# Loading the bias rows of all but the last pair of neighbourhood heads during the window heads

## The chip, the cores and the metric

The kernel runs on one core of one Trainium2 chip, in one launch. The metric is the device time of the launch in microseconds, the median of several executions. A profiled execution of the same kernel gives the trace; its own time and the span of its core (first to last instruction) are given below.

## What is computed

A trunk of two layers over 512 tokens of width 1024, float32 throughout. Each layer projects the normalised tokens once and feeds two kinds of attention heads, eight of each: heads of kind A (a window of blocks along the sequence, two heads of keys, rotary positions) and heads of kind B (each token looks at a neighbourhood of the 8 x 64 grid, with a learned bias by relative position). The change touches only how the bias of kind B reaches the chip.

```
def neighbourhood_attn(q, k, v, rel_bias):
    ...
    bias = rel_bias[:, dr_i[:, None, None, :, None], dc_i[None, :, :, None, :]]
    bias = jnp.where(valid[None, None, :, :, None, :], bias.astype(jnp.float32), NEG)
    ...
    scores = jnp.einsum('brjqhd,brjwkhd->bhrjqwk', qg, kb).astype(jnp.float32) * (HEAD_DIM ** -0.5)
    scores = scores + bias[None]
    ...
    p = jax.nn.softmax(scores.reshape(shp[:-2] + (wr * B_KBAND_C,)), axis=-1).reshape(shp)
    out = jnp.einsum('bhrjqwk,brjwkhd->brjqhd', p.astype(v.dtype), vb)

for l in range(DEPTH):
    h = rms_norm(x, attn_norm_g[l])
    z = jnp.einsum('bsd,dc->bsc', h, w_in[l])
    qa, ka, va, qb, kb, vb, ga, gb = jnp.split(z, IN_SPLITS, axis=-1)
    ...
    mixed = jax.nn.sigmoid(ga) * ya + jax.nn.sigmoid(gb) * yb
    x = x + jnp.einsum('bsd,de->bse', mixed, w_out[l])
    ...
    x = x + jnp.einsum('bsf,fd->bsd', u, w_down[l])
```

## The kernel before

Every product is split into a high and a low part of each operand and made of three matmuls of the type float32r. TensorE therefore has long rows of matmuls of the projections (tiles named `mm`, one PSUM bank each), and between them stand the short matmuls and transposes of the heads (tiles named `at`). All buffers in SBUF are cut from two arenas, one for float32 and one for float32r, so the profile knows them only as `arena`.

The order of the instructions is found when the program is built. The function `layer` yields one small unit of projection matmuls after another, and after each unit a driver may advance one of several generators ("chains"): one for each pair of heads (`chain_pair_a`, `chain_pair_b`), one for each head (`chain_heads`, which calls `head`). A chain goes on when its `Need` is met: given keys have been set, and by a planner's clocks the operands are ready. Each engine then carries out its own list strictly in that order. Since all calls go through one recording helper, nearly every row of the profile bears line L305.

The steps that matter here:

- `k_parts` makes the keys of a pair of heads. Two casts on ScalarE and two subtractions on VectorE (64 x 512 each) write the high and low keys of each head in half of the partitions, and four DMA issued by SyncE copy them to the other half (`arena<-arena`, 64 x 512, 128 KB each). The first score matmuls of a head wait for its two copies. It is called once for all heads of kind A, and once for each pair of kind B, so there are five groups of four copies in a layer.
- `bias_load` brings the bias of one head with 16 DMA issued by SyncE, of 8 KB each, so a pair takes 32 (`arena<-in_rel_bias_b`). A completion semaphore of SyncE's DMA is shared by every eighth one, so each of them waits until the one eight places ahead has landed.
- `bias_mask` adds the mask to the loaded bias with three additions on VectorE, when the head begins.

SyncE issues its DMA in the order of the program: a copy that stands behind a row of bias loads is issued only after the last of them. In this kernel the first pair's bias is requested at the end of the last pair of kind A, and each further pair's right behind the copies of keys of the pair ahead of it. `biases` is a list with one entry in it at a time.

Of the kernel before, what the change touches and what calls it, by code (L numbers as in the profile page):

```python
# [209 lines left out]
def trunk(ctx: ExitStack, tc: tile.TileContext, a: dict, out: bass.AP, lay: Layout):  # L210
# [20 lines left out]
    def buf(shape, dtype=F32):  # L231

        n = int(np.prod(shape))
        x = lay.place(n, dtype)
        t = arenas[dtype][:, x : x + n]
        if len(shape) == 2:
            t = t.rearrange("p (a b) -> p a b", b=shape[1])
        elif len(shape) == 3:
            t = t.rearrange("p (a b c) -> p a b c", b=shape[1], c=shape[2])
        return t  # L240
# [4 lines left out]
    def act(dtype=F32):  # L245
        return buf([S], dtype)
# [727 lines left out]
    def q_parts(tiles, col, res, scale=None):  # L974

        yield Need("pe", tiles, [at_slots])
        ps = turned(tiles, col, ident) if scale is None else turned_back(tiles, col)
        for own, other in HALVES:
            yield Need("act", [ps])
            q = act(F32R)  # L980
            if scale is None:
                yield from gsplit(held(ps[own]), by_columns(q[own]), by_columns(q[other]))
            else:
                yield from gsplit(ps[own], q[own], q[other], scale=scale[own])
            res.append(q)
        at_slots.give(clock["dve"])

    def k_parts(tiles, col, perm, res, in_a=False):

        dst, src = (by_columns, held) if in_a else (lambda t: t, lambda t: t)  # L990
        yield Need("pe", tiles, [at_slots])
        ps = turned(tiles, col, perm)
        for own, other in HALVES:
            yield Need("act", [ps])
            kh, kl = act(F32R), act(F32R)
            yield from gsplit(src(ps[own]), dst(kh[own]), dst(kl[own]))
            res.append((kh, kl))
        at_slots.give(max(clock["dve"], clock["act"]))
        for (own, other), (kh, kl) in zip(HALVES, res[-2:]):
            yield Need("dma", [kh, kl])  # L1000
            Q.dma_start(kh[other].bitcast(F32), kh[own].bitcast(F32))
            Q.dma_start(kl[other].bitcast(F32), kl[own].bitcast(F32))

    def v_parts(src, v):

        yield from gsplit(src, v[:, :, TOP], v[:, :, BOT])
# [117 lines left out]
    def bias_load(l, h):  # L1124

        t = buf([8, 32])
        src = a["rel_bias_b"]
        base = (l * 8 + h) * 15 * BW + 8
        for half in range(2):
            for r in range(8):  # L1130
                p = 64 * half + 8 * r
                Q.dma_start(
                    t[p : p + 8],
                    bass.AP(tensor=src.tensor, offset=base + r * BW + 8 * half, ap=[[1, 8], [BW, 8], [1, 32]]),
                )
        return t

    def bias_mask(t):

        bm = buf([2, 2, S // 4])  # L1140
        for i, n, k0 in ((0, 2, 0), (2, 1, 1), (3, 1, 0)):
            o = bm.rearrange("p e k (a n) -> p (e k a) n", n=64)[:, 2 * i : 2 * (i + n)]
            m = cst[:, C_MB + 16 * i : C_MB + 16 * (i + n)].rearrange("p (d c) -> p d c", c=8)
            b = t[:, :, 16 * k0 : 16 * (k0 + n)].rearrange("p r (d c) -> p d r c", c=8)
            V.tensor_tensor(
                o.rearrange("p d (r c) -> p d r c", c=8), b, m.unsqueeze(2).to_broadcast([P, 2 * n, 8, 8]), ALU.add
            )
        return lambda j: bm[:, int(j == 0)].rearrange("p k n -> p (k n)")
# [28 lines left out]
    def layer(l):  # L1177
# [68 lines left out]
        def chain_pair_a(hp):  # L1246

            keys = [f"qa{l}", f"ka{l}"] + ([f"{key}scores{2 * hp - 3}"] if hp > 1 else [])
            yield Need(keys=keys)
            qs = []  # L1250
            yield from q_parts(qa, P * hp, qs)
            oa.append(act())
            for i in range(2):
                h = 2 * hp + i

                def make(res, h=h, i=i, o=oa[-1]):
                    res += [
                        qs[i], k_a[h // 4], v_a[h // 4], mask_a, ident, nsnk[:, l, h : h + 1],
                        snk[:, l, h : h + 1], o[HALVES[i][0]], True,
                    ]  # L1260
                    yield Need()

                makes[h] = make
            if hp == 3:
                biases.append([bias_load(l, i) for i in range(2)])
            done.add(f"{key}pair{hp}")

        biases = []

        def chain_norm_b(half):  # L1270
            yield Need(keys=[f"qk{l}{half}"])
            f = []
            yield from head_scale(qk[half], 8, nrm.rst, f)
            for b in range(NB):
                yield Need()
                normalise(qk[half][b], f[0], b, 8)
            done.add(f"{key}norm{half}")

        def chain_pair_b(hp):

            g0 = 8 + 2 * hp
            raw, col = qk[hp // 2], P * (hp % 2)
            keys = [f"v{l}", f"{key}norm{hp // 2}", f"{key}scores{g0 - 3}"]
            if hp:
                keys += [f"{key}bias{g0 - 1}"]
            yield Need(keys=keys)
            rb = biases.pop()
            qs, ks = [], []
            yield from q_parts(raw, col, qs, scale=gb[:, l : l + 1])
            yield from k_parts(raw, 4 * HD + col, ident, ks)  # L1290
            if hp < 3:
                biases.append([bias_load(l, 2 * hp + 2 + i) for i in range(2)])
            ob.append(act())
            for i in range(2):
                h = 2 * hp + i

                def make(res, h=h, i=i, o=ob[-1]):
                    v = buf([NB, P], F32R)
                    yield Need("dve", [rb[i]])
                    bias = bias_mask(rb[i])  # L1300
                    done.add(f"{key}bias{8 + h}")
                    yield Need("act")
                    yield from v_parts(vb[:, :, HD * h : HD * h + HD], v)
                    res += [qs[i], ks[i], v, bias, rev, 3e38, None, o[HALVES[i][0]], False]
                    yield Need()

                makes[8 + h] = make
            done.add(f"{key}pair{4 + hp}")
# [28 lines left out]
        for hp in range(4):  # L1337
            spawn(chain_pair_a(hp))
            spawn(late(2 * hp))
            spawn(late(2 * hp + 1))  # L1340
        for hp in range(4):
            if hp % 2 == 0:
                spawn(chain_norm_b(hp // 2))
            spawn(chain_pair_b(hp))
            spawn(late(8 + 2 * hp))
            spawn(late(9 + 2 * hp))
# [317 lines left out]
    def main():  # L1664
        norms[0] = Norm(0)
        for l in range(DEPTH):
            yield from layer(l)
# [30 lines left out]
```

## Time and profile before

| what | value |
|---|---|
| median of 3 runs | 1421.5 us (1421.42 to 1421.89) |
| profiled execution, its own time | 1419.06 us |
| its span, mean granted TensorE clock | 1417.3 us, 0.993 |
| TensorE (PE) busy | 1382.1 us, 98% |
| VectorE (DVE) busy | 915.5 us, 65% |
| ScalarE (ACT) busy | 697.9 us, 49% |
| GpSimd (POOL) busy | 317.7 us, 22% |
| DMA issued by SyncE, share of 16 engines | 15.5% |
| DMA issued by GpSimd (weights), share of 16 engines | 54.1% |

In the views, times are microseconds from the span's start. A row of the timeline gives start, length, engine, operation, tiles and count, and in brackets how long the engine stood idle before it and what ended that. A row of the table of windows gives the window, its length, then the busy time (and count of instructions) of PE, PEld, DVE, ACT and POOL, the granted TensorE clock as a share of full speed, the busy share of the DMA engines, and GB/s. A row of the waits gives who waited for whom, the total, how often, and the longest. SPq is SyncE's queue, POOLq that of GpSimd.

### The profile page before, as it was taken

How to read it: one execution, taken by the hardware profiler on the slowest of the kernel's cores; microseconds unless marked ns; L12 is line 12 of the kernel's file. 1: busy time of each engine (PE TensorE's matmuls, PEld its weight loads, DVE VectorE, ACT ScalarE, POOL GpSimd, SP SyncE). 2: the span in 40 equal slices, each digit the busy share in tenths (PEclk: the TensorE clock that was granted, in tenths of full speed). 3: DMA queues.
4: the chain of work that ended last, by engine and by line, in shares of the span. 5: the costliest groups of instructions: out<-in, count | busy, mean ns of one | idle time of the engine just before them, and what ended most of it. 6: DMA issues, size and time to landing. Idle time of an engine off the chain costs nothing.

```text
span 1417.3 us, 20945 instructions
## 1 busy us (share of the span) xinstructions
PE 1382.1 (98%) x8042; PEld 1214.8 (86%) x8042; DVE 915.5 (65%) x1720; ACT 697.9 (49%) x1153; POOL 317.7 (22%) x326
## 2 busy tenths in 40 slices
PE   7999998999999999999999999899999999999998
PEld 5788886888899999999987888788888999999997
DVE  5876786455877566575648768683559657565653
ACT  6376765543654343333444766574347433343441
POOL 4442221320121111101343422123002210111110
PEclk9999998999999999999999999999999999999999
DMA  8877877994486465736799778779757584745645
GB/s 208 169 146 141 144 140 127 163 223 149 89 182 146 119 145 133 178 81 127 146 195 189 129 131 146 141 142 204 177 134 128 126 207 91 179 105 133 133 91 119
DMA packets 197332, 207.46 MB, mean 146 GB/s; under 512 B 25568, under 2 KB 167056, under 8 KB 197232
## 3 DMA queue, kind: packets, MB, share of 16 engines
q0 software_dynamic: 134976, 141.54, 54.1%
q1 hardware_dynamic: 61904, 64.04, 15.5%
q8 instruction: 63, 1.03, 0.3%
q10 hardware_dynamic: 352, 0.54, 0.1%
q14 instruction: 37, 0.30, 0.1%
HBM read 193.51 MB, written 2.10 MB: 138 GB/s over the span
## 4 chain that ended last, share of the span: by engine, by line
PE 78%; DVE 10%; DMA 5%; ACT 3%; issue 2%; SPq 1%; POOL 0%; DVEq 0%; POOLq 0%; ACTq 0%
PE mm L305 61%; PE at L305 17%; DVE arena L305 7%; ACT arena L305 3%; DMA arena<-in_rel_bias_b 2%; DVE sm L305 2%; DMA arena<-arena 1%; DMA arena<-in_w_in 1%; SPq L305 1%; DMA cst<-in_consts 0%; POOL arena L305 0%; DVE den L305 0%; DVE hf L305 0%; ACT L305 0%; POOL posi L305 0%
## 5 line engine op out<-in xcount | busy, mean ns | idle before, releaser
L305 PE MATMUL mm<-arena 128*128 128x512 f32 (+1 forms) x5568 | 1114.5, 356 | 6.0 <-DVE arena L305 3.1
L305 PEld LDWEIGHTS mm<-arena 128*128 128x128 f32 x5568 | 905.9, 190 | 140.4 <-DVE arena L305 5.7
L305 ACT CAST arena<-arena 128x1024 fp32r<-128x1024 f32 (+2 forms) x278 | 235.5, 869 | 203.2 <-DVE arena L305 190.0
L305 PE MATMUL at<-arena 128*128 128x256 f32 (+1 forms) x1952 | 288.7, 291 | 14.2 <-DMA arena<-arena 10.3
L305 DVE TENSOR_TENSOR arena<-arena,arena 128x1024 fp32r<-128x1024 f32 (+2 forms) x268 | 262.8, 994 | 61.1 <-ACT arena L305 59.9
L305 PEld LDWEIGHTS at<-arena 128*128 128x128 f32 x1952 | 262.6, 193 | 33.2 <-DMA arena<-arena 11.6
L305 ACT ACTIVATE arena<-arena 128x1024 fp32r<-128x1024 f32 (+3 forms) x252 | 206.6, 843 | 168.7 <-DMA arena<-in_w_down 81.7
L305 DVE TENSOR_TENSOR arena<-arena,mm 128x512 f32<-128x512 f32 x144 | 98.8, 686 | 231.4 <-PE mm L305 231.4
L305 POOL DMA_DIRECT2D arena<-in_w_in x163 | 162.5, 1409 | 345.7 <-ACT arena L305 334.3
L305 POOL DMA_DIRECT2D arena<-in_w_down x96 | 98.2, 1226 | 501.5 <-ACT arena L305 358.3
L305 DVE TENSOR_TENSOR arena<-arena 128x1024 f32<-128x1024 f32 (+4 forms) x196 | 158.4, 823 | 2.3
L305 DVE TENSOR_TENSOR arena<-at,arena 128x512 fp32r<-128x512 f32 (+4 forms) x158 | 103.1, 659 | 29.3 <-ACT arena L305 24.0
L305 ACT CAST arena<-at 128x512 fp32r<-128x512 f32 (+2 forms) x116 | 64.0, 554 | 95.8 <-PE at L305 72.1
L305 PE MATMUL at<-cst,arena 128*128 128x128 f32 x472 | 75.6, 280 | 4.8 <-DVE arena L305 4.3
L305 DVE TENSOR_TENSOR arena<-mm,arena 128x512 f32<-128x512 f32 x72 | 49.3, 688 | 45.7 <-PE mm L305 45.6
L305 ACT ACTIVATE arena<-arena,negm 128x256 f32<-128x256 f32 (+1 forms) x128 | 68.2, 534 | 13.5 <-DVE negm L305 12.4
L305 PEld LDWEIGHTS at<-cst,arena 128*128 128x128 f32 x472 | 58.2, 143 | 17.4 <-DVE arena L305 5.5
L305 ACT COPY arena<-at 128x512 f32<-128x512 f32 (+1 forms) x68 | 39.5, 581 | 61.2 <-PE at L305 60.4
L305 DVE CUSTOM_DVE_ANT_0 arena<-at,cst,nsnk 128x256 f32<-128x256 f32 (+1 forms) x64 | 34.6, 547 | 36.5 <-PE at L305 36.0
L305 ACT ACTIVATE arena<-arena,vecT 128x512 fp32r<-128x512 f32 x24 | 17.4, 726 | 53.0 <-DVE arena L305 52.6
L305 DVE CUSTOM_DVE_ANT_0 arena<-at,arena 128x256 f32<-128x256 f32 x64 | 26.3, 420 | 25.7 <-PE at L305 25.4
L305 DVE TENSOR_SCALAR arena<-arena,sm 128x256 f32<-128x256 f32 (+1 forms) x106 | 35.9, 397 | 1.1
(68 smaller groups left out, 392.6 us busy)
## 6 DMA issues: line engine op xcount, KB each, us to landing
arena<-in_w_in POOLq DMA_DIRECT2D x99, 512.0 KB, 7.3
arena<-in_w_down POOLq DMA_DIRECT2D x80, 512.0 KB, 6.8
arena<-in_w_gate SPq DMA_DIRECT2D x20, 1024.0 KB
arena<-in_w_up SPq DMA_DIRECT2D x20, 1024.0 KB
arena<-in_w_in POOLq DMA_DIRECT2D x64, 256.0 KB, 6.3
arena<-in_w_proj_a POOLq DMA_DIRECT2D x16, 512.0 KB, 7.5
arena<-in_w_proj_b POOLq DMA_DIRECT2D x16, 512.0 KB, 8.6
arena<-in_w_out SPq DMA_DIRECT2D x16, 512.0 KB
```

The costliest lines, as they stand in the source:

```text
L305: f(*args, **kw)
```

## The change

`chain_pair_a` now requests the bias of pair `hp` of kind B at the end of each of the first three pairs of kind A, and `chain_pair_b` requests the bias of the fourth pair behind the copies of the first. `biases` holds all four entries and is read by index. The bias buffers live longer for that, and since the arenas are packed by lifetime, many buffers get other addresses.

```diff
                 makes[h] = make
-            if hp == 3:
-                biases.append([bias_load(l, i) for i in range(2)])
+            if hp < 3:
+                bias_pair(hp)
             done.add(f"{key}pair{hp}")

         biases = []

+        def bias_pair(hp):
+            biases.append([bias_load(l, 2 * hp + i) for i in range(2)])
+
...
-            rb = biases.pop()
+            rb = biases[hp]
             qs, ks = [], []
             yield from q_parts(raw, col, qs, scale=gb[:, l : l + 1])
             yield from k_parts(raw, 4 * HD + col, ident, ks)
-            if hp < 3:
-                biases.append([bias_load(l, 2 * hp + 2 + i) for i in range(2)])
+            if hp == 0:
+                bias_pair(3)
```

The SyncE queue of the first layer, from the copies of the keys of kind A to the first weights of the output projection, stands like this in the kernel before:

```order
L305 DMA arena_73<-arena_73 64x512 x4
L305 DMA arena_72<-in_rel_bias_b 8x8x32 x32
L305 DMA arena_73<-arena_73 64x512 x4
L305 DMA arena_72<-in_rel_bias_b 8x8x32 x32
L305 DMA arena_73<-arena_73 64x512 x4
L305 DMA arena_72<-in_rel_bias_b 8x8x32 x32
L305 DMA arena_73<-arena_73 64x512 x4
L305 DMA arena_72<-in_rel_bias_b 8x8x32 x32
L305 DMA arena_73<-arena_73 64x512 x4
L305 DMA arena_72<-in_w_out 128x4x256 x8
```

The same stretch of the SyncE queue in the changed kernel, in which the number behind the x is again how many stand in a row:

```order
L305 DMA arena_73<-arena_73 64x512 x4
L305 DMA arena_72<-in_rel_bias_b 8x8x32 x96
L305 DMA arena_73<-arena_73 64x512 x4
L305 DMA arena_72<-in_rel_bias_b 8x8x32 x32
L305 DMA arena_73<-arena_73 64x512 x12
L305 DMA arena_72<-in_w_out 128x4x256 x8
```

The loads of the second and third pair have moved ahead of the first pair's copies, those of the fourth pair have moved up to right behind these, and the last three groups of copies follow each other with nothing between. The second layer has the same rows.

On the SyncE queue at the first of these places, with the semaphores that each DMA waits for (DMAHW are those of DMA issued by SyncE, DMASW of DMA issued by GpSimd), the kernel before has the four copies of kind A and the first bias load:

```order
L305 DMA arena_73<-arena_73 64x512 [waits DMASW1_49,DMAHW5_49,DMASW0_49,Activation_49]
L305 DMA arena_73<-arena_73 64x512 [waits DMAHW6_49,DVE_49]
L305 DMA arena_73<-arena_73 64x512 [waits DMAHW7_49,Activation_49]
L305 DMA arena_73<-arena_73 64x512 [waits DMAHW0_49,DVE_49]
L305 DMA arena_72<-in_rel_bias_b 8x8x32 [waits DMAHW1_49,DVE_49,Activation_49]
```

And the same five rows of the SyncE queue in the changed kernel:

```order
L305 DMA arena_73<-arena_73 64x512 [waits DMAHW5_49,Activation_49]
L305 DMA arena_73<-arena_73 64x512 [waits DMAHW6_49,DVE_49]
L305 DMA arena_73<-arena_73 64x512 [waits DMASW6_49,DMAHW7_49,PE_49,Activation_49]
L305 DMA arena_73<-arena_73 64x512 [waits DMAHW0_49,DVE_49]
L305 DMA arena_72<-in_rel_bias_b 8x8x32 [waits DMAHW1_49]
```

What moved is the first bias load's own wait: it no longer waits for VectorE and ScalarE to release its buffer, only for the DMA eight places ahead.

On TensorE the place is the begin of the third pair of kind B in the first layer: the transposes of the head ahead (`at` from `cst`), six projection matmuls, the first two score matmuls (`at`, 128 x 256), projection matmuls again, and the next head matmuls. Before:

```order
L305 MATMUL at_2174<-cst,arena_72 128x128
L305 MATMUL mm_2008<-arena_73 128x512 x6
L305 MATMUL at_2191<-arena_73 128x256 x2
L305 MATMUL mm_2008<-arena_73 128x512 x3
L305 MATMUL at_2199<-arena_73 128x256 x4
```

And TensorE at the same place in the changed kernel:

```order
L305 MATMUL at_2174<-cst,arena_72 128x128
L305 MATMUL mm_2040<-arena_73 128x512 x6
L305 MATMUL at_2191<-arena_73 128x256 x2
L305 MATMUL mm_2040<-arena_73 128x512 x3
L305 MATMUL at_2199<-arena_73 128x256 x4
```

Only numbers in names differ. That holds for the whole lists of TensorE, VectorE, ScalarE and GpSimd: the same instructions in the same order, with other addresses. Only SyncE's list is in another order.

## The prediction, made before the changed kernel ran

> **What bounds the kernel now.** First the page's busy shares, then PE's own waits, because an idle microsecond counts only on the engine that sets the end.
>
> ```profile
> PE 1382.1 (98%) x8042; PEld 1214.8 (86%) x8042; DVE 915.5 (65%) x1720; ACT 697.9 (49%) x1153; POOL 317.7 (22%) x326
> PE at L305 <- DMA arena<-arena: 10.3, 4, 4.0
> PE at L305 <- DVE arena L305: 6.4, 12, 1.5
> ```
>
> TensorE is the bound, idle for about 35 of 1417 us. The largest single reason in its waits is four waits on the copies of keys. PE's timeline says where they are, two in each layer, at the first scores of the third pair of kind B:
>
> ```profile
> 212.06 1.64 PE L305 MATMUL mm<-arena 128*128 128x512 f32 x6
> 217.73 0.58 PE L305 MATMUL at<-arena 128*128 128x256 f32 x1 [4.03 <-DMA arena<-arena]
> 220.44 0.58 PE L305 MATMUL at<-arena 128*128 128x256 f32 x1 [2.13 <-DMA arena<-arena]
> ...
> 908.87 0.38 PE L305 MATMUL at<-arena 128*128 128x256 f32 x1 [0.35 <-DMA arena<-arena]
> 913.01 0.58 PE L305 MATMUL at<-arena 128*128 128x256 f32 x1 [3.76 <-DMA arena<-arena]
> ```
>
> Why are the copies late? SyncE's timeline answers (layer 0, then the rows of layer 1 that matter):
>
> ```profile
> 68.83 3.34 SPq L305 DMA_DIRECT2D arena<-arena  x4
> 93.39 13.61 SPq L305 DMA_DIRECT2D arena<-in_rel_bias_b  x32
> 147.32 5.82 SPq L305 DMA_DIRECT2D arena<-arena  x4
> 153.18 19.72 SPq L305 DMA_DIRECT2D arena<-in_rel_bias_b  x32
> 187.00 3.58 SPq L305 DMA_DIRECT2D arena<-arena  x4
> 190.67 19.82 SPq L305 DMA_DIRECT2D arena<-in_rel_bias_b  x32
> 212.17 4.26 SPq L305 DMA_DIRECT2D arena<-arena  x4
> 216.47 15.12 SPq L305 DMA_DIRECT2D arena<-in_rel_bias_b  x32
> 235.11 5.21 SPq L305 DMA_DIRECT2D arena<-arena  x4
> ...
> 767.42 18.97 SPq L305 DMA_DIRECT2D arena<-in_rel_bias_b  x32
> 842.21 5.82 SPq L305 DMA_DIRECT2D arena<-arena  x4
> 885.51 19.55 SPq L305 DMA_DIRECT2D arena<-in_rel_bias_b  x32
> 905.23 5.27 SPq L305 DMA_DIRECT2D arena<-arena  x4
> ```
>
> The third pair's copies (212.17, 905.23) follow a row of 32 bias loads with almost no gap; the first, second and fourth groups (147.32, 187.00, 235.11) come after SyncE had been free for 40, 14 and 3.5 us, so those wait for their data. The data of the third group were there long before, which ScalarE's cast and VectorE's subtraction of its first head show, for each layer:
>
> ```profile
> 200.94 0.58 ACT L305 CAST arena<-at 64x512 fp32r<-64x512 f32 x1
> 202.00 0.68 DVE L305 TENSOR_TENSOR arena<-at,arena 64x512 fp32r<-64x512 f32 x1
> ...
> 895.81 0.58 ACT L305 CAST arena<-at 64x512 fp32r<-64x512 f32 x1
> 896.87 0.68 DVE L305 TENSOR_TENSOR arena<-at,arena 64x512 fp32r<-64x512 f32 x1
> ```
>
> High and low keys are ready at 201.52 and 202.68 (896.39, 897.55), and the copies are issued 10.6 and 10.1 us later (8.8 and 9.7 in layer 1, at 905.23 and 907.20, below). The chain of waits runs the same way, from a bias load into a copy into PE (last row: layer 1):
>
> ```profile
> 205.74 6.35 DMA arena<-in_rel_bias_b
> ...
> 212.74 7.65 DMA arena<-arena
> 220.39 0.04 issue
> 220.44 0.58 PE at L305
> ...
> 907.20 5.77 DMA arena<-arena
> ```
>
> The wait has a tail. The windows from the last matmul before it to where PE is at speed again, in each layer, and the rest of the heads behind it:
>
> ```profile
> 213.70:220.44 6.74, 0.59 (x3) 0.29 (x2) 0.34 (x2) 0.00 (x0) 0.00 (x0) 0.66 1.30 227
> 220.44:226.20 5.76, 5.76 (x21) 5.18 (x22) 2.50 (x8) 1.90 (x6) 0.00 (x0) 0.51 0.21 21
> 226.20:264.70 38.50, 38.50 (x217) 32.91 (x217) 30.32 (x82) 27.35 (x62) 10.30 (x10) 1.00 0.75 135
> 908.50:913.00 4.50, 0.40 (x2) 0.19 (x1) 0.35 (x2) 0.00 (x0) 0.00 (x0) 0.91 1.21 220
> 913.00:919.10 6.10, 6.09 (x22) 5.51 (x23) 2.50 (x8) 2.23 (x8) 0.00 (x0) 0.51 0.48 84
> ```
>
> Behind each wait PE runs some 6 us at a granted clock of 0.51, fully busy. [...]
>
> **The change part by part.**
>
> *Bias loads of the third pair out of the way of the third copies.* In the changed queue they stand ahead of the first copies, and behind the second copies (issued by 190.6) nothing stands before the third. These are issued when their data are: about 201.6 and 202.7. A copy's flight is not known for that moment; the rows give 7.65 us as a long one, and in SyncE's rows a group of four with its issues takes as little as 3.34. At the long end the low keys land at 210.4, while PE has its projection matmuls until 213.70. In layer 1: 897.6 + 7.65 = 905.2 against 908.5. So the wait goes in both layers, with 3.3 us to spare at the worst, and without an idle gap there is no slow tail.
>
> Layer 0: the two windows are 6.74 + 5.76 = 12.50 us. Their work at full clock is 5.76 x 0.51 = 2.94, and the one matmul of the first window at half of 0.59, 0.30: 3.24. Saved: 9.26. Layer 1: 4.50 + 6.10 = 10.60; work 0.40 + 6.09 x 0.51 = 3.51. Saved: 7.09. Together 16.35 us.
>
> *What is late next.* During the wait VectorE and ScalarE ran dry too (0.34 and 0.00 us of work in 6.74), but at 213.70 they had at most that 0.34 us left, so the pause gave them no lead that PE would miss. Behind it VectorE is busy 30.32 of 38.50 us (79%) and PE waits for nothing. If VectorE's 0.34 + 2.50 us must be done in 3.24 us instead of 12.5, it is 88% busy there, and a wait of some tenths may come. Between 0 and the 0.44 us of the longest such wait near here I take 0.2 in each layer: 16.35 - 0.4 = about 16.0 us.
>
> ```profile
> 191.45 0.62 PE L305 MATMUL at<-arena 128*128 128x256 f32 x3 [0.44 <-DVE arena L305]
> ```
>
> From there to the end of the span the lists of PE, DVE, ACT and POOL are unchanged, so what PE gains is kept if weights keep pace; GpSimd issues them in an order tied to ScalarE's instructions, which move up with PE.
>
> *96 bias loads in a row behind the copies of kind A.* Same number, same bytes, other time. They begin when these copies are issued, 72.2 us (no other wait on the first), and go at 13.61/32 = 0.43 to 19.82/32 = 0.62 us each, which is 41 to 60 us. They end between 113 and 132 us; the first pair's copies need the queue at 147.32, so 15 us are free. Layer 1: 767.4 + 60 = 827 against 842.2. Cost 0.
>
> *Fourth pair's loads behind the first copies.* They take the place of the second pair's loads there, 32 for 32 (153.18 to 172.9), ahead of 187.00. Cost 0.
>
> *Earlier traffic beside the weights.* Landing times of weight loads while 32 bias loads run (window 93 to 113), then without them (113 to 147):
>
> ```profile
> q1 hardware_dynamic: 2304, 0.26, 12.1%
> ...
> arena<-in_w_in POOLq DMA_DIRECT2D x10, 256.0 KB, 7.2
> ...
> arena<-in_w_in POOLq DMA_DIRECT2D x2, 256.0 KB, 5.6
> ```
>
> 32 loads take 12.1% of 20 us of all engines, 2.4 us; 96 take 7.3, of which 4.8 are new in this stretch. Weights land 1.6 us later beside them. PE's waits name no weight transfer in either layer's heads, though three such rows of loads already run there. So between 0 and 4.8 us per layer I take 0, the value of the three rows observed. The traffic leaves the stretch from 190 us on, where it could only help; I count 0 for that as well.
>
> *Longer lives of bias buffers.* New addresses mean new releases to wait for; the lists show such waits on SyncE for weights of the output projection and the feed-forward part, which are requested well ahead. Priced at 0; bounded by the 0.44 us row per place.
>
> **Sum.** 16.0 us against the profiled 1419.06 us gives 1403.1. The median of the runs stands 2.4 us above the profiled execution, so I forecast 1421.5 - 16.0 = 1405.5 us.
>
> **Rivals.**
>
> 1. *The gap closes only in part, or the tail stays.* If the third copies were late for another reason (a flight above 11 us), only part of the wait goes. If the idle goes and the slow clock remained, the gain is the idle alone: 4.03 + 2.13 + 0.35 + 3.76 = 10.3 us, 1411.2. Against it: clock 1.00 in the windows without a gap.
>
> 2. *Weights arrive late under the 96 loads.* By the bound above up to 4.8 us per layer: 1405.5 + 9.6 = 1415.1 at most, 1408 to 1412 if half or less shows. For it: 7.2 against 5.6 us. Against: no such wait beside 32. [...]
>
> 3. *Slower: the first copies queue behind the 96 loads.* The mechanism that is removed at the third pair would return at the first, whose scores PE reaches at 166.72 in layer 0:
>
> ```profile
> 166.72 0.40 PE L305 MATMUL at<-arena 128*128 128x256 f32 x2
> ```
>
> Allowing 7.65 us of flight, the queue must be free by 159. It becomes late from (159 - 72.2)/96 = 0.90 us a load, and eats the whole gain of 8 us per layer from 0.99. At 1.1 us a load it would cost 19 us per layer and end at 1421.5 - 16 + 38 = 1443. Each load waits for the landing of the eighth ahead, so 0.99 means landings near 8 us; the observed rate of 0.62 means about 5. The loads would have to slow each other by 60%, and eight are in flight in either kernel.
>
> 4. *No change.* The third copies would have to be as late as before, or VectorE would have to hold PE at the same place. At 81 to 88% of VectorE I see no 8 us for that. 1421.5.
>
> **How the numbers follow.** Forecast 0.78, with a range of its own from 1404 to 1408; rival 1 0.06; rival 2 0.08; rival 3 0.04; no change 0.04. Faster by over 0.2% (2.8 us, about what a measurement here can tell from no change) are the forecast and rivals 1 and 2, 0.92. Within 0.2%: 0.05, no change and a mild case of rival 3. Slower: 0.03. The low end 1403.5 is the full 16.35 with no new wait and somewhat freer DMA; the high end 1411 takes in most of rivals 1 and 2. Outside lie rivals 3 and 4 and the rest of 1 and 2, under 0.2.
>
> **What would show it.** In the changed profile: no wait of PE on `arena<-arena` above 0.5 us; the third group of copies issued near 201.6 and 896, each 2 to 8 us after its cast; clock 1.00 from 213 to 226 and from 908 to 919; the heads' last matmuls about 9 us earlier in layer 0 and 16 in layer 1; 96 bias loads from about 72 to 113 to 132 us. Wrong would be: copies of the first pair issued later than 148 us behind bias loads, PE waiting for `in_w_in` between 72 and 150, or a new wait of PE on VectorE of over 1 us behind 214.

## The result, and the profile after

| | before | changed |
|---|---|---|
| median | 1421.7 us (1421.42 to 1422.44, 4 runs) | 1402.99 us (1402.83 to 1403.64, 4 runs) |
| profiled execution | 1419.06 us | 1402.89 us |
| its span | 1417.3 us | 1401.1 us |
| granted clock over the span | 0.993 | 0.999 |

The ratio is 0.9868 (95% interval 0.9851 to 0.9886), a gain of 18.7 us in the median, where 16.0 was forecast. The change does what its steps said, at the places that they named. Its worth in an ordinary execution was forecast too small: 1402.99 us came where 1405.5 was forecast. That size is what most of the runs below are about.

First the page's busy shares and PE's waits of the changed kernel, of which the first three rows are quoted:

```profile
PE 1377.6 (98%) x8042; PEld 1210.4 (86%) x8042; DVE 914.9 (65%) x1720; ACT 697.4 (50%) x1153; POOL 317.2 (23%) x326
...
PE at L305 <- DVE arena L305: 5.9, 12, 1.5
PE at L305 <- DMA vec<-in_ffn_norm_g: 4.5, 1, 4.5
PE mm L305 <- ACT arena L305: 1.7, 2, 1.3
```

The row on the copies of keys, 10.3 us before, is gone. PE's busy time fell too, by 4.5 us with the same 8042 matmuls, since those behind the waits ran at a granted clock of 0.51 in the kernel before and run at 1.00 here. SyncE's timeline (layer 0, and the first loads of layer 1) shows the queue without the loads in the way:

```profile
67.81 3.34 SPq L305 DMA_DIRECT2D arena<-arena  x4
71.20 50.51 SPq L305 DMA_DIRECT2D arena<-in_rel_bias_b  x96
146.27 5.82 SPq L305 DMA_DIRECT2D arena<-arena  x4
152.14 19.65 SPq L305 DMA_DIRECT2D arena<-in_rel_bias_b  x32
...
757.52 51.78 SPq L305 DMA_DIRECT2D arena<-in_rel_bias_b  x96
```

The 96 loads run from 71.2 to 121.7 us, 0.53 us each, and end 24.6 us before the first copies' data are there. The third group of copies by itself, behind the cast of its high keys (SyncE, ScalarE), and PE's and the windows' rows at the place where PE used to wait:

```profile
199.86 0.58 ACT L305 CAST arena<-at 64x512 fp32r<-64x512 f32 x1
...
200.46 6.23 SPq L305 DMA_DIRECT2D arena<-arena  x4
...
212.47 0.40 PE L305 MATMUL at<-arena 128*128 128x256 f32 x2
212.70 0.86 PE L305 MATMUL mm<-arena 128*128 128x512 f32 x3
...
212.63:216.00 3.37, 3.37 (x24) 3.06 (x24) 2.65 (x8) 1.50 (x5) 0.00 (x0) 1.00 1.20 219
898.92:905.00 6.08, 6.08 (x41) 5.43 (x39) 4.22 (x16) 4.07 (x11) 0.67 (x1) 1.00 0.86 166
```

The first copy is issued 0.02 us after its cast ends. The two score matmuls at 212.47 have no bracket, so PE did not wait; it is busy for all of the windows at clock 1.00, in both layers.

### The profile page after: what moved, and what is told of

Read it like the earlier page. It is cut to its first block, busy times and chain, and to the rows that moved or that the text cites. A ratio compares the mean times of both kernels' runs of the same rounds, so it can differ in the third digit from the quotient of the medians.

```text
span 1401.1 us, 20895 instructions
## 1 busy us (share of the span) xinstructions
PE 1377.6 (98%) x8042; PEld 1210.4 (86%) x8042; DVE 914.9 (65%) x1720; ACT 697.4 (50%) x1153; POOL 317.2 (23%) x326
## 4 chain that ended last, share of the span: by engine, by line
PE 77%; DVE 9%; issue 4%; DMA 4%; ACT 3%; POOL 2%; SPq 0%; DVEq 0%; ACTq 0%; POOLq 0%
PE mm L305 60%; PE at L305 17%; DVE arena L305 7%; ACT arena L305 3%; DMA arena<-in_w_in 2%; DVE sm L305 2%; POOL arena L305 1%; DMA arena<-in_rel_bias_b 1%; DMA snk<-in_sink_a 0%; DMA arena<-arena 0%; DMA posi<-in_positions 0%; SPq L305 0%; ACT mm L305 0%; POOL gqa L305 0%; DVE hf L305 0%
## 5 line engine op out<-in xcount | busy, mean ns | idle before, releaser
L305 PE MATMUL at<-arena 128*128 128x256 f32 (+1 forms) x1952 | 285.6, 290 | 4.1 <-DVE arena L305 2.1
L305 POOL DMA_DIRECT2D arena<-in_w_up x8 | 8.2, 1030 | 117.4 <-PE mm L305 69.8
```

The source lines that it names most:

```text
L305: f(*args, **kw)
```

## The experiments

All were timed against the kernel before; every kernel here has the same instructions in the same order on PE, VectorE, ScalarE and GpSimd as the kernel before, save for the extra matmuls of `e6_keep_busy`.

### What an ordinary execution of the kernel before looks like

No edit: the kernel before, profiled once more.

> The kernel before, unchanged, for a second profile. The changed kernel gained 18.7 us in the median, while the sum made from the profile gave 16.0 (16.35 without the allowance for VectorE), and the profiled execution of before was itself 2.4 us faster than the median of its runs. Theory A: the missing 2.4 us are in the same two stalls, which vary from execution to execution; in a profile that took 1421.5 the two stretches from the last matmul ahead of the third copies to the clock's return measure about 25.5 us together instead of 23.1. Theory B: they are outside the attention heads (start of the launch, or weights), and the two stretches again measure 23.1 within 0.3.

Measured: 1422.19 us (ratio 1.0003, 0.9994 to 1.0012); its 19 executions as the reference beside this kernel ran from 1414.34 to 1424.4 us. The profiled one took 1422.86. PE's waits on the copies, and the windows of its two stalls and the slow stretches behind them:

```profile
PE at L305 <- DMA arena<-arena: 13.6, 4, 4.0
...
213.04:220.15 7.11, 0.58 (x2) 0.29 (x2) 0.34 (x2) 0.00 (x0) 0.00 (x0) 0.67 1.19 216
220.15:225.93 5.78, 5.78 (x22) 5.20 (x22) 2.50 (x8) 1.91 (x6) 0.00 (x0) 0.52 0.20 21
908.35:916.04 7.69, 0.58 (x1) 0.29 (x1) 0.34 (x2) 0.00 (x0) 0.00 (x0) 0.72 1.08 201
916.04:922.15 6.11, 6.11 (x22) 5.53 (x23) 2.50 (x8) 2.24 (x8) 0.00 (x0) 0.51 0.15 21
```

The stretches sum to 26.69 us in place of 23.10, 3.6 more in an execution that took 3.8 more. Theory A stands. Most of it is in layer 1, where both copies came late here (3.98 and 3.14 us) and only one in the first profile (0.35 and 3.76). The chain of waits has the reason for the second: the copy of the low keys took 8.53 us from issue to landing in place of 5.77.

```profile
907.47 8.53 DMA arena<-arena
```

### One part alone: the third pair's loads

```diff
-            if hp == 3:
-                biases.append([bias_load(l, i) for i in range(2)])
+            if hp > 1:
+                bias_pair({2: 2, 3: 0}[hp])
...
-            if hp < 3:
-                biases.append([bias_load(l, 2 * hp + 2 + i) for i in range(2)])
+            if hp in (0, 2):
+                bias_pair({0: 1, 2: 3}[hp])
```

> One part of the change alone: only the loads of the third pair move (to the end of the third pair of kind A); those of the first, second and fourth pairs stay where the kernel before has them. Theory: the whole gain is the third copies' wait, so 1403.0 within 1.0, and PE has no wait on the copies of keys. Rival: what exceeds the sum (2.7 us) comes from the other moved loads or from calmer DMA; then about 1405.5.

Measured: 1404.54 us, ratio 0.9879 (0.9865 to 0.9894). By its time alone it misses the 1403.0 within 1.0 of the theory and is nearer to the rival's 1405.5. The spans decide: 1400.9 to 1401.9 in its four executions against 1401.0 to 1401.6 in the four of the whole change. So the 1.5 us lie outside the time from the first to the last instruction; what they are stays open. PE has no wait on copies. Within the span, the third pair's loads alone are the gain.

### All of the change but that part

```diff
-            if hp == 3:
-                biases.append([bias_load(l, i) for i in range(2)])
+            if hp < 2:
+                bias_pair(hp)
...
-            if hp < 3:
-                biases.append([bias_load(l, 2 * hp + 2 + i) for i in range(2)])
+            if hp < 2:
+                bias_pair({0: 3, 1: 2}[hp])
```

> The change without the part that the sum rests on: loads of the first two pairs run during the heads of kind A and those of the fourth behind the first copies, but those of the third pair stay behind the second copies, ahead of the third. Theory: 1421.5 within 1.0, four waits of PE on the copies of keys as before. Rival (other moved loads bring the 2.7 us): about 1419.

Measured: 1421.17 us, ratio 0.9999 (0.9986 to 1.0013): no gain, as the theory has it. Its profiled execution was a short one, 1417.57 us, with three waits of PE on copies, where the theory had four, and these windows:

```profile
PE at L305 <- DMA arena<-arena: 9.6, 3, 5.0
...
213.18:217.49 4.31, 0.39 (x3) 0.19 (x2) 0.34 (x2) 0.00 (x0) 0.00 (x0) 1.00 1.17 211
217.49:223.00 5.51, 5.51 (x24) 4.97 (x25) 2.80 (x11) 1.84 (x6) 0.00 (x0) 0.69 0.51 86
905.39:911.48 6.09, 0.39 (x2) 0.19 (x2) 0.28 (x1) 0.00 (x0) 0.00 (x0) 0.93 1.29 225
911.48:917.60 6.12, 6.12 (x22) 5.54 (x23) 2.50 (x8) 2.25 (x8) 0.00 (x0) 0.51 0.06 11
```

Here the stretches sum to 22.03 us. So the length of the same two stalls differs from 22.0 to 26.7 us in three profiles, with the time of the execution.

### Rival 3 at work: the loads doubled

The first of two kernels gives each of the first three pairs a second set of loads into buffers that nobody reads.

```diff
         def bias_pair(hp):
-            biases.append([bias_load(l, 2 * hp + i) for i in range(2)])
+            biases[hp] = [bias_load(l, 2 * hp + i) for i in range(2)]
+            if hp < 3:
+                spare.append([bias_load(l, 2 * hp + i) for i in range(2)])
```

> The changed kernel with each of the first three pairs loaded twice (the second time into buffers that nobody reads), so 192 loads stand ahead of the first copies. Theory of one queue in order: at 0.53 us a load, as the changed kernel shows (50.5 us for 96), the queue is free at 71 + 101 = 172 instead of 122; the first copies are issued then instead of at 146 and land at 175 to 178; PE, which needs them at 165.5, waits 10 to 12 us and loses 2.5 us to the slow clock, 13 us per layer: 1429, between 1422 and 1436. If loads slow each other to 0.62 us, the queue is free at 190 and the time is near 1460. If the order on the queue did not matter: 1403.

Measured: 1506.71 us, ratio 1.06 (1.0578 to 1.0621), and not by the mechanism expected. The timelines of ScalarE and VectorE:

```profile
102.15 0.51 ACT L305 ACTIVATE arena<-arena,negm 128x256 f32<-128x256 f32 x1 [20.36 <-DMA arena<-in_rel_bias_b]
121.47 1.15 ACT L305 ACTIVATE arena<-arena 128x512 f32<-128x512 f32 x2 [14.38 <-DMA arena<-in_rel_bias_b]
...
101.62 0.48 DVE L305 CUSTOM_DVE_ANT_0 arena<-at,cst,nsnk 128x256 f32<-128x256 f32 x1 [21.80 <-DMA arena<-in_rel_bias_b]
122.14 0.69 DVE L305 TENSOR_REDUCE sm<-arena 128x8 f32<-128x512 f32 x1 [14.32 <-DMA arena<-in_rel_bias_b]
```

A buffer that nobody reads is free for the planner as soon as its load has ended by the planner's clock, which knows nothing of the row of loads on SyncE. Its place is given to the heads of kind A, and these wait for loads far back in the queue. (The waits are in the trace; that reuse is their reason is read from the program.) The loads took 81.75 us, 0.43 us each, and ended at 153.3, while the first copies were issued only at 196.63, so these did not wait for the loads. So the price here is that of reuse, and the run says nothing on rival 3. The second kernel loads twice into the same buffer:

```diff
-        for half in range(2):
-            for r in range(8):
+        for half, r in times * [(half, r) for half in range(2) for r in range(8)]:
```

> The changed kernel with each load of the first three pairs issued twice into the same buffer, so that 192 loads stand ahead of the first copies and no other buffer is touched. The queue in order: at 0.43 us a load (as 192 took in the run with spare buffers) it is free at 71 + 82 = 153, the first copies land at about 160 and PE, which needs them at 165.5, does not wait: 1403. At 0.53 us (as 96 took in the changed kernel) it is free at 172, the copies land near 179, PE waits 14 us and loses 2.5 to the clock in each layer: 1436. What is read is the rate, the end of the loads and whether PE's wait on the copies follows it. In the run with spare buffers the time came from ScalarE and VectorE waiting for loads into buffers that were planned as free; here no such wait is expected.

Measured: 1439.23 us, ratio 1.0125 (1.0088 to 1.0162). SyncE's rows, and PE's waits in the two layers:

```profile
71.15 107.22 SPq L305 DMA_DIRECT2D arena<-in_rel_bias_b  x192
178.54 2.39 SPq L305 DMA_DIRECT2D arena<-arena  x4
...
180.82 1.22 PE L305 MATMUL at<-arena 128*128 128x256 f32 x2 [14.96 <-DMA arena<-arena]
...
884.35 1.28 PE L305 MATMUL at<-arena 128*128 128x256 f32 x2 [14.71 <-DMA arena<-arena]
```

The loads go at 0.56 us each, a little slower than either rate that was expected, and end at 178.4. The copies follow at once, and PE waits 14.96 and 14.71 us for them, which with the slow clock behind makes 36 us against the changed kernel. That is rival 3 as it was described: 192 loads at 0.56 us fill the time of 96 at 1.12. The prediction gave 19 us per layer at 1.1, and by the same working 21 at 1.12; 18 were measured. It had allowed 7.65 us for the copies, and here PE goes on 2.3 us after the first of them is issued. Rival 3 did not come in the change because 96 loads need 50.5 us of the 75 that are there.

### The slow clock by itself

The kernel before, with matmuls that nobody reads in the place of the idle time:

```diff
             ps = at_bank()
+            if g == 12 and j == 0 and not lay.dry:
+                for _ in range(WARM):
+                    nc.tensor.matmul(ps, q[:, :P], q, start=True, stop=True, skip_group_check=True)
             mm(ps[:, :n], q[:, P * j : P * j + P], keys(kh, j), True, False)
```

> The kernel before with 26 matmuls of 128 x 512 that nobody reads (0.227 us each, 5.9 us) on TensorE ahead of the first scores of the third pair of kind B in each layer, where it waits for the late copies. It separates the idle time from the slow clock behind it. Theory (the clock falls because TensorE stands idle): granted clock 1.00 behind the place, the two tails of 2.8 and 3.0 us go, up to 1.5 us is lost where the extra matmuls last longer than the wait: 1415.7 to 1417.2. Rival (the tail is refilling the engines behind a stall, not the clock): 1421.5 or slower.

Measured: 1417.0 us, ratio 0.9969 (0.9956 to 0.9982), beside 1422.42 for the kernel before on the same chip: 5.4 us. PE's timeline and the windows behind the place in both layers:

```profile
212.89 6.08 PE L1068 MATMUL at<-arena 128*128 128x512 f32 x26
220.22 0.38 PE L306 MATMUL at<-arena 128*128 128x256 f32 x1 [1.14 <-DMA arena<-arena]
...
221.00:227.00 6.00, 6.00 (x39) 5.36 (x38) 4.10 (x15) 4.51 (x12) 1.22 (x2) 1.00 0.20 22
915.00:921.00 6.00, 6.00 (x40) 5.36 (x39) 4.29 (x14) 4.75 (x13) 1.52 (x2) 1.00 0.18 22
```

The copies land about as late as before (PE's last wait on them ends at 220.22 and 913.92 us, in the kernel before at 220.44 and 913.01), PE is kept busy for most of that time, and the clock stays at 1.00; the short gaps that are left, up to 1.14 us, do not bring it down. So it is the long idle time, waits of up to 4.03 and 3.76 us, that brought it to 0.51 in the kernel before. The 5.4 us agree with the 5.8 that the windows gave the two tails, but the interval of the ratio reaches from 2.6 to 6.3 us, so the time alone fixes the price of the tails only roughly; that they are the clock's is shown by the rows. (Here a real kernel would rather not wait at all.)

### All four pairs early, and the changed kernel again

```diff
-            if hp < 3:
-                bias_pair(hp)
+            bias_pair(hp)
...
-            if hp == 0:
-                bias_pair(3)
```

> All four pairs loaded during the heads of kind A, so 128 loads in a row. One queue in order: at 0.53 us they end at 71 + 68 = 139, ahead of the first copies' data at 146: the time of the changed kernel, 1403 within 0.7. If ScalarE or VectorE has to wait for buffers: slower by their wait.

Measured: 1403.29 us, ratio 0.9872 (0.9849 to 0.9895). 128 loads take 67.03 us and end at 138.6, still ahead of the copies; the time is that of the changed kernel.

> The changed kernel once more beside the others. Theory A (before's executions differ in the two waits alone): its executions lie within 1.5 us of each other, while those of before spread over 10 us. Theory B (the spread has another source): the same spread in both.

Measured: 1402.84 us, ratio 0.987 (0.9843 to 0.9898), its four executions from 1402.53 to 1403.43; the 13 of the kernel before beside it from 1416.1 to 1423.63, a spread of 7.5 us. The spread of the kernel before goes with the waits, as theory A has it. No kernel here beats the changed one.

## Why the prediction was right or wrong, point by point

- **The cause.** Right: the third copies stood behind 32 bias loads. `e2_third_only` has the whole gain, `e3_all_but_third` none.
- **The third copies in time.** Right: issued at 200.46 with the cast, needed at 212.47, no wait.
- **The sum against the profiled execution.** Right within the small terms of the next point but one: 1419.06 - 16.35 = 1402.7 without the allowance for VectorE, 1403.1 with it; measured 1402.99. That it fits to some tenths is in part luck, as the lead of this execution below shows. The same working on the other two profiles gives the same end. `e1_before_again`: work at full clock 5.78 x 0.52 + 0.29 + 6.11 x 0.51 + 0.29 = 6.7, so 26.69 - 6.7 = 20.0 saved, 1422.86 - 20.0 = 1402.9. `e3_all_but_third`: work 0.39 + 5.51 x 0.69 + 0.39 + 6.12 x 0.51 = 7.7, so 22.03 - 7.7 = 14.3 saved, 1417.57 - 14.3 = 1403.2.
- **From the profiled execution to the median.** Wrong; this is the step that failed. "The median of the runs stands 2.4 us above the profiled execution" was added to the result as if it were a constant around the program. It was not: the executions of the kernel before differ by what their two stalls last (three profiles: 14.3, 16.35, 20.0 us of loss), and a change that removes the stalls removes the difference. For the median execution the same working would have to give 18.7 us, which is what was measured, and the profile happened to show a milder one. The three profiles cover executions from 1417.57 to 1422.86 us; those outside, down to 1414.34 and up to 1424.4, have no trace. The range's low end of 1403.5 rested on the same step and lay 0.5 us too high.
- **What is late next.** Right in kind, too small. PE's rows at the same instructions of the two profiles, the kernel before (first five) and the changed one, tell what was gained and given back:

```profile
226.26 0.86 PE L305 MATMUL mm<-arena 128*128 128x512 f32 x3
235.21 0.49 PE L305 MATMUL at<-arena 128*128 128x256 f32 x2
...
906.87 1.64 PE L305 MATMUL mm<-arena 128*128 128x512 f32 x6
920.50 2.31 PE L305 MATMUL mm<-arena 128*128 128x512 f32 x9
925.20 0.60 PE L305 MATMUL at<-cst,arena 128*128 128x128 f32 x4
```

```profile
210.99 1.64 PE L305 MATMUL mm<-arena 128*128 128x512 f32 x6
215.72 0.85 PE L305 MATMUL mm<-arena 128*128 128x512 f32 x3
225.44 0.48 PE L305 MATMUL at<-arena 128*128 128x256 f32 x2
...
897.28 1.64 PE L305 MATMUL mm<-arena 128*128 128x512 f32 x6
903.52 2.32 PE L305 MATMUL mm<-arena 128*128 128x512 f32 x9
908.71 0.66 PE L305 MATMUL at<-cst,arena 128*128 128x128 f32 x4
```

  Ahead of the place the changed kernel is 212.06 - 210.99 = 1.07 us early, from the start of the launch, which the change does not touch. Behind it the lead is 10.54, so layer 0 gained 9.47 (9.26 forecast), and nine microseconds later 9.77: 0.77 is given back. In layer 1 the lead goes from 9.59 to 16.98, a gain of 7.39 (7.09 forecast), and to 16.49, 0.49 given back. At the end of the span it is 16.2. So 1.3 us are given back in the dense stretches behind the place in place of the 0.4 allowed, and 0.5 elsewhere; PE's waits name nobody for it. That it is VectorE is not shown: over the nine microseconds behind the place in layer 0, VectorE is busy for 7.21 of 9.72 us, no denser than the 6.75 of 8.95 before (and the prediction's "81 to 88%" begins too high: its row gives 30.32 of 38.50, 79%). The early start of this one execution, 1.07 us, and the gain of 16.86 in place of 16.35 at the two places covered what was given back; that is luck.
- **96 loads in a row, rival 2, rival 3.** Right that all cost nothing here. The rate was 0.53 us within the forecast 0.43 to 0.62. The median landing of weights was 1.1 us longer beside the loads, and PE waited for none of them:

```profile
arena<-in_w_in POOLq DMA_DIRECT2D x9, 256.0 KB, 6.5
...
arena<-in_w_in POOLq DMA_DIRECT2D x2, 256.0 KB, 5.4
```

  (the changed kernel, 93 to 113 us with loads, 113 to 147 mostly without). That a load waits until the one eight places ahead has landed, from which the prediction worked out its landings of 5 and 8 us, shows in the chain of waits of the kernel before:

```profile
197.35 5.95 DMA arena<-in_rel_bias_b
203.30 0.02 issue
203.32 0.28 SPq L305
```

  The load issued at 197.35 us lands at 203.30, and the eighth behind it is issued at 203.32. `e5_twice_in_place` shows the mechanism of rival 3 and its price at 1.12 us a load; where between 0.53 and 1.12 it begins, no run shows.
- **The slow tail, rival 1.** Right as a term of its own. `e6_keep_busy` removes the tail and fills most of the wait with matmuls that nobody reads, and gains 5.4 us where the windows priced the two tails at 5.8.

## What to carry to other kernels

SyncE's queue issued in order here, and the small urgent copies waited for every bulk load ahead of them: 32 loads in 19.82 us in the kernel before, 192 in 107.22 us in `e5_twice_in_place`. So bulk loads whose data are known early belong where the queue is idle, and the room there is counted in loads times the measured rate (96 at 0.53 us in 75 us here). When a stall is removed, forecast the absolute time from the profiled execution less its own stalls, and do not add back the distance to the median: the stalls may be what makes executions differ. A wait of TensorE of 3.7 us or more for the third copies cost its length and, behind it, 1.7 us (a clock of 0.69 over 5.51 us, `e3_all_but_third`) to 3.0 us (0.51 over 6.10 us, the kernel before); the gaps of up to 1.14 us in `e6_keep_busy` had no such stretch behind them.

## What the hardware showed unexpectedly

- The flight of the same copy of keys (64 x 512, between two halves of SBUF) differed from execution to execution: 5.77 us in the kernel before and 8.53 in `e1_before_again` for the low keys of the third pair in layer 1. The busy share of the DMA engines was 1.21 and 1.08 in the windows of these two stalls; what sets the length was not tried.
- The half clock begins inside the wait (in layer 0 of `e3_all_but_third` at its end: 1.00 over the wait, 0.69 over the 5.51 us behind it). In the kernel before, PE stands idle from 213.70, the clock falls from 1.00 to 0.50 at 215.9 and is back at 226.1:

```profile
215.00:215.90 0.90, 0.00 (x0) 0.00 (x0) 0.00 (x0) 0.00 (x0) 0.00 (x0) 0.98 1.24 200
216.10:226.10 10.00, 6.25 (x21) 5.37 (x22) 2.50 (x8) 1.80 (x6) 0.00 (x0) 0.50 0.71 120
226.10:226.40 0.30, 0.30 (x4) 0.30 (x3) 0.00 (x0) 0.30 (x3) 0.00 (x0) 0.98 0.18 27
```

  The clock that the trace records is 0.50 for 10.24 and 6.83 us in the two layers here. From the windows of the other two profiles (twice the missing share of the clock times the length) the time at half speed is 10.2 and 10.3 us in `e1_before_again`, 3.4 and 6.8 in `e3_all_but_third`. These six lie near one, two and three times 3.4 us; no run shows why. What lies behind the end of the wait, and so slows PE's work, is 5.5 to 6.0 us in five of the six cases and 3.4 in layer 0 of `e3_all_but_third` (5.51 x 0.31 / 0.5). In `e5_twice_in_place`, behind a wait of 14.96 us, PE's rows are slow for about 3.6 us in layer 0: three projection matmuls take 1.49 us at 181.84, and nine take 2.23 again at 185.71.
